# Depthwise convolution of two channel tiles by even and odd tokens, and adaLN sums in PSUM

## The chip, the cores and the metric

The kernel is written by hand for one core of a Trainium2 chip; the seven others are idle. The metric is the device time of one execution in microseconds (us). The core has a matrix engine (PE), a vector engine (DVE), an activation engine (ACT), a general engine (POOL) and a queue engine (SP), each with its own in-order instruction stream; they wait for each other by semaphores. SBUF is the on-chip memory of 128 partitions; PSUM is the smaller memory that PE writes, here eight banks of 128 x 512 fp32.

## The reference

One layer of a decoder trunk on 1024 tokens of width 1024, all in fp32:

```python
mod = silu(c) @ ada_w + ada_b                      # 1024 -> 6 x 1024
sh1, sc1, g1, sh2, sc2, g2 = split(mod, 6)
h = rms_norm(x, mix_pre_g) * (1 + sc1) + sh1
proj = h @ w_in          # q, k, v: 512 each; 8 gate logits; conv value, conv gate: 512 each
attn = fox_attention(q, k, v, log_sigmoid(f_logit + b_f))
u = conv_val * sigmoid(conv_gate)
u = causal_depthwise_conv(u, conv_w, conv_b)       # 31 taps, per channel, over tokens
u = silu(layer_norm(u, conv_ln_g, conv_ln_b))      # over the 512 channels
y = concat([attn, u]) @ w_o
x = x + g1 * rms_norm(y, mix_post_g)
h = rms_norm(x, ffn_pre_g) * (1 + sc2) + sh2
x = x + g2 * rms_norm(swiglu_ffn(h), ffn_post_g)   # 1024 -> 2 x 2816 -> 1024
```

The change touches the depthwise convolution and the first line, the product of one vector with the wide matrix `ada_w`.

## The kernel before

Channels lie on the partitions, tokens along the free axis. Every matrix product is three matmuls of two-part operands (`mm3`, L322 to L325): high times high, low times high, high times low. The parts are made by ACT (`whi`, L306) and DVE or POOL (`wlo`, `hTl`, L307).

The first 70 us follow a hand-written list of steps (`SEQ`, L37) that fixes the order on all five queues. In it the tokens are loaded, normalised and transposed (`xhat`, `ptx`), and the scale and shift of adaLN are made by column tiles of 128, for `j` from 0 to 7. `ada_load` brings a 128 x 8 x 2 x 128 piece of `ada_w` from DRAM through SP. `ada_sum` multiplies each of the 8 slices with a number per partition and adds them up on DVE into one or two running sums `adac` (L227, L229). `ada_turn` adds the partitions up by matmuls with a column of ones (`pada`, L239), and two small DVE operations make `acol` and `bcol`. With them ACT scales a tile of `h`, which is split and fed to the first projection matmuls (`pg`).

Then PE makes the projections: conv gate and value of channel tiles 1, 2, 3 (`conv_tile`, each gate and value tile two halves of 512 tokens), v, then k and q (`kq`), each into one of the five PSUM banks of `gbank`. Between conv tiles 1 and 2 stands `ada_row` (L283): the row form of the gate g1 in two halves of 512, each a sum of 8 slices on DVE (`adacr`, L196 and L198), one matmul with ones that sums the partitions (`padar`, L297) and two DVE operations into `g1b` (L299, L300).

The conv of a channel tile is 31 taps on two halves of 512 tokens (`conv_unit`): `csum += w[j] * u[j : j + 512]`. Of the eight units three are done by ACT (product `ctmp`, L413) and POOL (sum, L416) and five by DVE: a first product (L406) and 30 more operations (L409), whose running sum `csum` is one PSUM bank; the last tap writes the result `cacc` to SBUF. DVE's taps are given the lowest priority (`later`), so that the scheduler places them in gaps between other DVE work. POOL's and ACT's orders are by hand in this stage; those of DVE, PE and SP come from priorities.

From the projection of the last k and q tiles on, `conv_norm` transposes the four `cacc` of 128 tokens into a bank (`ptl`, L673), takes the statistics (`bs`, L676), aggregates them (`mv`, L678), makes the reciprocal deviation on POOL (L680) and normalises on DVE (`xn`, L682). `conv_silu` transposes back (`ptm`, L689). The banks of `ptl`, `ptm`, `ptx`, `padar` and `ptf` are the two of `tbank`. `ptf` (L563) transposes `lt`, the log of the forget gates, ahead of the second half of v, whose low parts DVE writes into `vv` (L593: per token and head 64 values, then 64 of the high part). The adaLN columns of the FFN (`ada_cols`, tiles `aacc`) are summed in the same stage in SBUF. Attention, `w_o` and the FFN follow and are not touched by the change, but that the FFN's `ada_row` uses the edited helper `ada_acc`.

## Time and profile before

| | us |
|---|---|
| runs | 1238.88, 1247.13, 1244.58 |
| median | 1244.58 |
| the profiled execution, its own time | 1241.7 |
| its span | 1239.8 |
| PE busy in the span | 1152.4 (93%) |
| DVE busy | 901.5 (73%) |
| POOL busy | 730.3 (59%) |
| ACT busy | 578.3 (47%) |

The span is the stretch of the profiled execution in which the engines worked; the execution's own time is 1.9 us longer, and the median of the runs is 2.9 us above it. The busy shares are means over stages of very different kinds: the first 70 us, the projections up to about 303 us, attention up to 445 us, then `w_o` and the FFN. The mean granted clock of PE is 0.973 of full speed.

### The profile page before, as it was taken

What the parts mean: (1) busy time and instruction counts of PE and PEld (TensorE: products, weight loads), DVE (VectorE), ACT (ScalarE), POOL (GpSimd) and SP (SyncE); (2) the same over time, 40 slices, a digit from 0 to 9 for tenths busy, and PEclk for the clock granted to TensorE, in tenths of its full rate; (3) what the DMA queues carried; (4) which work ended last, traced back from release to release, by engine and by line L of the source; (5) the groups of instructions that cost most, each with busy time, mean ns of one, the idle gap of its engine ahead of it and who ended that gap; (6) DMA issues with size and microseconds to landing.
All of it is one profiled execution on the core that took longest, in us unless ns stands there. A gap on an engine that the chain in (4) does not pass through costs nothing.

```text
span 1239.8 us, 16349 instructions
## 1 busy us (share of the span) xinstructions
PE 1152.4 (93%) x5517; PEld 949.1 (77%) x5517; DVE 901.5 (73%) x1395; ACT 578.3 (47%) x1084; POOL 730.3 (59%) x653
## 2 busy tenths in 40 slices
PE   4898989987799999898999999999999999999886
PEld 4676888876689977786788888888888877867565
DVE  4869899897598844548875656676665557597996
ACT  4654665363688845545433333333333244433451
POOL 3667878865667624565655545545455255456864
PEclk9999999988899999998899999999999999999999
DMA  9663102875966356412332332332313591444041
GB/s 300 178 221 86 35 18 70 233 236 173 287 176 168 100 167 196 136 51 89 119 119 69 98 103 81 124 98 81 102 56 107 191 358 46 157 148 144 31 149 68
DMA packets 177292, 166.41 MB, mean 134 GB/s; under 512 B 9789, under 2 KB 139153, under 8 KB 177208
## 3 DMA queue, kind: packets, MB, share of 16 engines
q1 hardware_dynamic: 158800, 151.62, 39.5%
q10 hardware_dynamic: 17096, 9.02, 2.6%
q0 software_dynamic: 1312, 4.72, 1.1%
q8 instruction: 44, 0.72, 0.2%
q14 instruction: 40, 0.33, 0.1%
HBM read 129.64 MB, written 33.06 MB: 131 GB/s over the span
## 4 chain that ended last, share of the span: by engine, by line
PE 61%; DVE 18%; POOL 7%; DMA 6%; issue 4%; ACT 3%; SPq 0%; POOLq 0%; ACTq 0%; DVEq 0%
PE mm L324 12%; PE mm L325 12%; PE mm L323 12%; PE m L324 4%; DVE wlo L307 4%; PE m L325 3%; PE m L323 3%; DVE csum L409 3%; PE pv L908 2%; PE pt L882 2%; DVE adac L229 2%; POOL cacc L416 2%; ACT whi L306 1%; PE sp L826 1%; PE sp L822 1%
## 5 line engine op out<-in xcount | busy, mean ns | idle before, releaser
L1116 POOL TENSOR_TENSOR sm<-raw 128x512 f32<-128x512 f32 x108 | 149.2, 1399 | 111.6 <-DVE fwl L307 93.8
L307 DVE TENSOR_TENSOR wlo<-raw,whi 128x512 fp32r<-128x512 f32 (+2 forms) x99 | 118.5, 1197 | 60.4 <-ACT whi L306 60.3
L416 POOL TENSOR_TENSOR cacc<-cacc,ctmp 128x512 f32<-128x512 f32 x90 | 128.4, 1427 | 28.3 <-ACT ctmp L413 21.8
L306 ACT CAST whi<-raw 128x512 fp32r<-128x512 f32 (+2 forms) x99 | 82.4, 834 | 125.2 <-PE m L325 50.6
L324 PE MATMUL m<-wlo,whi 128*128 128x512 f32 (+1 forms) x292 | 119.0, 407 | 17.8 <-DVE wlo L307 17.5
L306 ACT CAST fwh<-sm 128x512 fp32r<-128x512 f32 (+1 forms) x86 | 62.9, 731 | 132.3 <-PE mm L324 94.8
L325 PE MATMUL m<-whi,wlo 128*128 128x512 f32 (+1 forms) x292 | 114.7, 393 | 0.0
L323 PE MATMUL m<-whi 128*128 128x512 f32 (+1 forms) x292 | 114.0, 393 | 0.1
L409 DVE SCALAR_TENSOR_TENSOR csum<-u,cw,csum 128x512 f32<-128x512 f32 x145 | 108.9, 751 | 3.2
L1319 POOL TENSOR_TENSOR u<-u,g 128x512 f32<-128x512 f32 x42 | 61.7, 1469 | 79.9 <-ACT fwh L306 59.3
L323 PE MATMUL mm<-hTh,whi 128*128 128x512 f32 x224 | 90.9, 406 | 0.2 <-ACT whi L306 0.2
L324 PE MATMUL mm<-hTl,whi 128*128 128x512 f32 x224 | 90.7, 405 | 0.0
L325 PE MATMUL mm<-hTh,wlo 128*128 128x512 f32 x224 | 89.5, 402 | 0.0
L324 PEld LDWEIGHTS m<-wlo,whi 128*128 128x128 f32 x292 | 54.7, 187 | 43.5 <-DVE wlo L307 32.4
L413 ACT ACTIVATE ctmp<-u,cw 128x512 f32<-128x512 f32 x90 | 64.0, 723 | 43.9 <-POOL cacc L416 43.8
L307 DVE TENSOR_TENSOR fwl<-sm,fwh 128x512 fp32r<-128x512 f32 (+1 forms) x86 | 77.0, 896 | 10.0 <-ACT fwh L306 9.9
L1398 POOL TENSOR_TENSOR raw<-ablk,a 128x512 f32<-128x512 f32 x33 | 55.3, 1674 | 35.8 <-DVE wlo L307 34.3
L323 PEld LDWEIGHTS m<-whi 128*128 128x128 f32 x292 | 54.9, 188 | 13.5 <-DVE u L1316 0.5
L325 PEld LDWEIGHTS m<-whi,wlo 128*128 128x128 f32 x292 | 54.9, 188 | 11.1
L198 DVE SCALAR_TENSOR_TENSOR adacr<-adawr,cact,adacr 128x128 f32<-128x128 f32 (+1 forms) x70 | 60.6, 875 | 1.6
L842 POOL TENSOR_TENSOR nm<-nm,ones_n 128x1 f32<-128x1 f32 x64 | 39.2, 613 | 32.1 <-ACT pm L836 26.9
L1318 ACT ACTIVATE g<-g 128x512 f32<-128x512 f32 x44 | 27.7, 630 | 61.0 <-DVE g L1311 55.9
(349 smaller groups left out, 3495.6 us busy)
## 6 DMA issues: line engine op xcount, KB each, us to landing
raw<-in_w_ffn_in_dram SPq DMA_DIRECT2D x44, 512.0 KB, 3.6
bblk<-in_w_ffn_out_dram SPq DMA_DIRECT2D x55, 256.0 KB, 2.8
act_d<-u SPq DMA_DIRECT2D x42, 256.0 KB, 2.5
raw<-in_w_in_dram SPq DMA_DIRECT2D x18, 512.0 KB, 5.4
ablk<-act_d SPq DMA_DIRECT2D x33, 256.0 KB, 3.0
xt<-in_x_dram SPq DMA_DIRECT2D x16, 512.0 KB, 5.6
adaw<-in_ada_w_dram SPq DMA_DIRECT2D x16, 512.0 KB, 7.4
adaw<-in_ada_w_dram ACTq DMA_DIRECT2D x16, 512.0 KB, 3.9
```

Source lines behind the costliest of these rows:

```text
L198: nc.vector.scalar_tensor_tensor(acc, w[:, a], cact[:, a : a + 1], acc, ALU.mult, ALU.add)
L306: nc.scalar.copy(hi, raw)
L307: eng.tensor_tensor(lo, raw, hi.bitcast(F32), ALU.subtract)
L323: nc.tensor.matmul(ps, sh, mh, start=first, stop=False)
L324: nc.tensor.matmul(ps, sh, ml, start=False, stop=False)
L325: nc.tensor.matmul(ps, sl, mh, start=False, stop=last)
L409: eng.scalar_tensor_tensor(ps if j < CK - 1 else acc, us, w, ps, ALU.mult, ALU.add)
L413: nc.scalar.activation(tmp, us, AF.Copy, scale=w)
L416: eng.tensor_tensor(acc, acc, tmp, ALU.add)
L1116: nc.gpsimd.tensor_tensor(d, blk[o[0]], blk[o[2]], o[1])
L1319: (nc.vector if f == NF - 1 else nc.gpsimd).tensor_tensor(u, u, g, ALU.mult)
L1398: eng.tensor_tensor(sm[:, zs], blocks[c + o[0], k], blocks[c + o[2], k], o[1])
```

## The change

Two things change.

Conv tiles 2 and 3 are done by `conv_pair`. For even and odd tokens, with `a` the even taps' filter (16 taps) and `b` the odd taps' filter (15 taps), a 31-tap result of 1024 tokens is made of three filters: `a` on one half of the tokens (`pa`), `b` on the other (`pb`), and `a + b` on the sum of the two halves (`csm`). Each of the first two reads every second token of `u`. The even outputs are `pa + pb`; the odd outputs are the third filter less the two, built up in PSUM with the negated sums of taps, `cwn`. The last token is done alone by a small operation. `csum` gets two banks, so the projections' `gbank` gets four instead of five.

The running sums of adaLN go to PSUM: `ada_sum`'s into the same two banks as `csum` (`arun`), where `pada` now lives too, and `ada_row`'s into a bank of `tbank` (`adar`). Only the last operation of each sum writes SBUF. The mask of the first stage shares the space of `g1b`, and one scratch tile has a single buffer.

```diff
--- before.py
+++ after.py
@@ -94,6 +94,8 @@
     C_MP, C_AB, C_FP, C_CB, C_LG, C_LB = 0, 8, 56, 64, 68, 72
     bfb = cst.tile([P, NH], F32, name="bfb")
     cw = cst.tile([P, 4, CK], F32, name="cw")
+    cwn = cst.tile([P, 4, CK // 2], F32, name="cwn")
+    cbn = cst.tile([P, 4], F32, name="cbn")
     vT = cst.tile([P, NV], F32, name="vT")
     ab1 = cst.tile([P, 48], F32, name="ab1")
     cact = cst.tile([P, NK], F32, name="cact")
@@ -107,7 +109,7 @@
     stp, stp_es = pool("stp", 2)
 
     def gbank(name):
-        return psI.tile([P, 512], F32, tag="mm", name=name, bufs=5)
+        return psI.tile([P, 512], F32, tag="mm", name=name, bufs=4)
 
     def tbank(name):
         return psT.tile([P, 512], F32, tag="tr", name=name, bufs=2)
@@ -116,7 +118,7 @@
     crow = stp.tile([NK, P], F32, name="crow", bufs=1)
     vrows = stp.tile([C_FP, P], F32, name="vrows", bufs=1)
     vrows2 = stp.tile([NV - C_FP, P], F32, name="vrows2", bufs=1)
-    mask32 = stp.tile([P, P], F32, name="mask32", bufs=1)
+    mask32 = g1b[:, :P]
     nc.gpsimd.memset(mask32, 0.0)
     nc.gpsimd.affine_select(
         out=mask32, in_=mask32, pattern=[[-1, P]], compare_op=ALU.is_ge,
@@ -164,6 +166,9 @@
             pt = tbank("ptc")
             nc.tensor.transpose(pt[:, :CK], cwr[:, cb * P : (cb + 1) * P], ident[:CK, :CK])
             nc.vector.tensor_copy(cw[:, cb, :], pt[:, :CK])
+        nc.vector.scalar_tensor_tensor(
+            cwn, cw[:, :, 0 : CK - 1 : 2], -1.0, cw[:, :, 1::2], ALU.mult, ALU.subtract)
+        nc.vector.tensor_scalar(cbn, vT[:, C_CB : C_CB + 4], -2.0, 0.0, ALU.mult, ALU.add)
 
 
     xhat = stp.tile([P, NT, D], F32, name="xhat", bufs=1)
@@ -179,7 +184,7 @@
     def x_load(t):
         xt = xts[t] = stp.tile([P, D], F32, tag="xt", name="xt", bufs=3)
         nc.sync.dma_start(xt, xd[t * P : (t + 1) * P, :])
-        jk = stp.tile([P, D], BF16, tag="jk", name="jk")
+        jk = stp.tile([P, D], BF16, tag="jk", name="jk", bufs=1)
         nc.scalar.activation(jk, xt, AF.Square, accum_out=ss[:, t : t + 1])
         rstd_of(rstd[:, t : t + 1], ss[:, t : t + 1], D)
 
@@ -191,11 +196,13 @@
             nc.gpsimd.tensor_scalar(xhat[:, t, :], xt, rstd[:, t : t + 1], 0.0, ALU.mult, ALU.add)
 
 
-    def ada_acc(w, acc):
-
-        nc.vector.tensor_scalar_mul(acc, w[:, 0], cact[:, 0:1])
+    def ada_acc(w, acc, run=None):
+
+        run = acc if run is None else run
+        nc.vector.tensor_scalar_mul(run, w[:, 0], cact[:, 0:1])
         for a in range(1, NK):
-            nc.vector.scalar_tensor_tensor(acc, w[:, a], cact[:, a : a + 1], acc, ALU.mult, ALU.add)
+            nc.vector.scalar_tensor_tensor(
+                run if a < NK - 1 else acc, w[:, a], cact[:, a : a + 1], run, ALU.mult, ALU.add)
 
     acol = cst.tile([P, 2, NK], F32, name="acol")
     bcol = cst.tile([P, 2, NK], F32, name="bcol")
@@ -220,18 +227,21 @@
 
         w, npe, na = aw[j], int('40100000'[j]), int('22212111'[j])
         acc = stp.tile([P, 2, 2, P], F32, tag="adac", name="adac", bufs=2)
+        run = psI.tile([P, 512], F32, tag="cs", name="arun", bufs=2).rearrange("p (z m n) -> p z m n", z=2, m=2)
         aacc[j] = acc, na
         for a in range(npe, NK):
-            d = acc[:, (a - npe) % na]
+            z = (a - npe) % na
+            d = run[:, z]
             if a - npe < na:
                 nc.vector.tensor_scalar_mul(d, w[:, a], cact[:, a : a + 1])
             else:
-                nc.vector.scalar_tensor_tensor(d, w[:, a], cact[:, a : a + 1], d, ALU.mult, ALU.add)
+                nc.vector.scalar_tensor_tensor(
+                    d if a + na < NK else acc[:, z], w[:, a], cact[:, a : a + 1], d, ALU.mult, ALU.add)
 
     def ada_turn(j):
         acc, na = aacc.pop(j)
         w, npe = aw.pop(j), int('40100000'[j])
-        pt = gbank("pada")
+        pt = psI.tile([P, 512], F32, tag="cs", name="pada", bufs=2)
         for m in range(2):
             ops = [(w[:, a, m, :], cact[:, a : a + 1]) for a in range(npe)] + [
                 (acc[:, z, m], onesf[:, 0:1]) for z in range(na)]
@@ -291,7 +301,7 @@
             nc.sync.dma_start(br[:, 1], gvec[0:1, h * n : (h + 1) * n].broadcast_to([P, n]))
             yield
             acc = pl.tile([P, n], F32, tag="adac", name="adacr", bufs=2)
-            ada_acc(w, acc)
+            ada_acc(w, acc, bank("adar")[:, :n])
             yield
             pt = bank("padar")
             nc.tensor.matmul(pt[:, :n], onesf, acc, start=True, stop=True)
@@ -396,7 +406,7 @@
 
         acc = cvp.tile([P, 512], F32, tag=f"ca{cb}{h}", name="cacc", bufs=1)
         cacc[cb, h] = acc
-        ps = psI.tile([P, 512], F32, tag="cs", name="csum", bufs=1) if eng is nc.vector else None
+        ps = psI.tile([P, 512], F32, tag="cs", name="csum", bufs=2) if eng is nc.vector else None
 
         def tap(j):
             def f():
@@ -419,7 +429,41 @@
         for j in range(CK):
             put(tap(j))
 
+    def conv_pair(cb, u):
+
+
+
+        acc = cvp.tile([P, S], F32, tag=f"cq{cb}", name="cacc", bufs=1)
+        for h in range(2):
+            cacc[cb, h] = acc[:, HF[h]]
+        N, M = S // 2, CK // 2
+        pa, pb = [psI.tile([P, 512], F32, tag="cs", name="csum", bufs=2) for _ in range(2)]
+        sm = cvp.tile([P, N + M - 1], F32, tag="csm", name="csm", bufs=1)
+        bias = vT[:, C_CB + cb : C_CB + cb + 1]
+        w = lambda j: cw[:, cb, j : j + 1]
+        at = lambda j, n=N: u[:, j : j + 2 * n - 1 : 2]
+        v = nc.vector
+        later(v.tensor_scalar, pa, at(0), w(0), bias, ALU.mult, ALU.add)
+        for j in range(2, CK, 2):
+            later(v.scalar_tensor_tensor, pa, at(j), w(j), pa, ALU.mult, ALU.add)
+        later(v.tensor_scalar, pb, at(1), w(1), 0.0, ALU.mult, ALU.add)
+        for j in range(3, CK, 2):
+            later(v.scalar_tensor_tensor, pb if j < CK - 2 else acc[:, 0::2], at(j), w(j), pb, ALU.mult, ALU.add)
+        later(v.tensor_tensor, sm, at(1, N + M - 1), at(2, N + M - 1), ALU.add)
+        pb = pb[:, : N - 1]
+        later(v.scalar_tensor_tensor, pb, pa[:, 1:], cbn[:, cb : cb + 1], acc[:, 0 : S - 2 : 2], ALU.add, ALU.add)
+        later(v.tensor_tensor, acc[:, 0::2], pa, acc[:, 0::2], ALU.add)
+        for i in range(M):
+            later(v.scalar_tensor_tensor, pb, sm[:, i : i + N - 1], cwn[:, cb, i : i + 1], pb, ALU.mult, ALU.add)
+        later(v.scalar_tensor_tensor, acc[:, 1 : S - 1 : 2], sm[:, M : M + N - 1], w(CK - 1), pb, ALU.mult, ALU.subtract)
+        jk = cvp.tile([P, CK], F32, tag="cjk", name="cjk", bufs=1)
+        later(lambda: v.tensor_tensor_reduce(
+            out=jk, in0=u[:, S - 1 : S - 1 + CK], in1=cw[:, cb, :], scale=1.0, scalar=bias,
+            op0=ALU.mult, op1=ALU.add, accum_out=acc[:, S - 1 : S]))
+
     def conv_taps(cb, u):
+        if cb >= 2:
+            return conv_pair(cb, u)
         for h in range(2):
             if (cb, h) in POOL_UNITS:
                 conv_unit(cb, h, u, nc.gpsimd, pool_work.append)
```

Three places in the order of the instructions follow. In the rows `mm` is a projection bank and `padar` the matmul that sums the partitions of an `adacr`; numbers behind names are tiles' numbers.

On PE, around the second `padar`; before, it stands in the second half of the gate projection of conv tile 2 (`mm_916`), 34 matmuls behind the first `padar`:

```order
L324 MATMUL mm_916<-hTl_100,whi_748 128x512
L325 MATMUL mm_916<-hTh_99,wlo_749 128x512
L323 MATMUL mm_916<-hTh_99,whi_748 128x512
L297 MATMUL padar_870<-adacr_861,onesf_77 128x512
L324 MATMUL mm_916<-hTl_100,whi_748 128x512
L325 MATMUL mm_916<-hTh_99,wlo_749 128x512
L323 MATMUL mm_916<-hTh_99,whi_748 128x512
```

With the change, in the first half of the value projection of conv tile 2 (`mm_970`), 55 matmuls behind the first:

```order
L334 MATMUL mm_970<-hTl_102,whi_913 128x512
L335 MATMUL mm_970<-hTh_101,wlo_914 128x512
L333 MATMUL mm_970<-hTh_101,whi_913 128x512
L307 MATMUL padar_883<-adacr_873,onesf_77 128x512
L334 MATMUL mm_970<-hTl_102,whi_913 128x512
L335 MATMUL mm_970<-hTh_101,wlo_914 128x512
L333 MATMUL mm_970<-hTh_101,whi_913 128x512
```

The second `padar` has moved 21 matmuls back; the first stands where it stood.

On DVE, from the second half of conv tile 1's `u` on, before: the second sum of `adacr` had begun ahead of it, with three of its eight operations done:

```order
L198 SCALAR_TENSOR_TENSOR adacr<-adawr,cact,adacr 128x512
L409 SCALAR_TENSOR_TENSOR csum<-u,cw,csum 128x512
L383 TENSOR_TENSOR u<-mm,sg 128x512
L299 TENSOR_TENSOR g1b<-padar,adab 128x512
L198 SCALAR_TENSOR_TENSOR adacr<-adawr,cact,adacr 128x512
L300 TENSOR_TENSOR g1b<-g1b,adab 128x512
L198 SCALAR_TENSOR_TENSOR adacr<-adawr,cact,adacr 128x512
L307 TENSOR_TENSOR wlo<-raw,whi 128x1024
L198 SCALAR_TENSOR_TENSOR adacr<-adawr,cact,adacr 128x512
L409 SCALAR_TENSOR_TENSOR csum<-u,cw,csum 128x512
L198 SCALAR_TENSOR_TENSOR adacr<-adawr,cact,adacr 128x512
L409 SCALAR_TENSOR_TENSOR csum<-u,cw,csum 128x512
```

With the change:

```order
L416 TENSOR_SCALAR csum<-u,cw,vT 128x512
L419 SCALAR_TENSOR_TENSOR csum<-u,cw,csum 128x512 x5
L393 TENSOR_TENSOR u<-mm,sg 128x512
L309 TENSOR_TENSOR g1b<-padar,adab 128x512
L202 TENSOR_SCALAR adar<-adawr,cact 128x512
L310 TENSOR_TENSOR g1b<-g1b,adab 128x512
L204 SCALAR_TENSOR_TENSOR adar<-adawr,cact,adar 128x512
L317 TENSOR_TENSOR wlo<-raw,whi 128x1024
L204 SCALAR_TENSOR_TENSOR adar<-adawr,cact,adar 128x512
L419 SCALAR_TENSOR_TENSOR csum<-u,cw,csum 128x512
L204 SCALAR_TENSOR_TENSOR adar<-adawr,cact,adar 128x512
L419 SCALAR_TENSOR_TENSOR csum<-u,cw,csum 128x512
```

The second sum (now `adar`) begins with its first product (L202) behind `u` and the first `g1b`; its remaining operations alternate with taps as before.

On DVE, at the end of the conv, before: the transposes' first statistics (`BN_STATS`) and what follows, with taps of the last tile behind them:

```order
L307 TENSOR_TENSOR wlo<-raw,whi 128x1024
L645 SCALAR_TENSOR_TENSOR tql<-mm,tq 128x512
L409 SCALAR_TENSOR_TENSOR csum<-u,cw,csum 128x512 x9
L632 TENSOR_TENSOR tl<-mm,th 128x512
L409 SCALAR_TENSOR_TENSOR csum<-u,cw,csum 128x512
L676 BN_STATS bs<-ptl 128x6 x2
L196 TENSOR_SCALAR aacc<-adaw_2385,cact 128x128
L678 BN_AGGR mv<-bs 128x2 x2
L198 SCALAR_TENSOR_TENSOR aacc<-adaw_2385,cact,aacc 128x128
L409 SCALAR_TENSOR_TENSOR csum<-u,cw,csum 128x512
```

With the change:

```order
L475 SCALAR_TENSOR_TENSOR csum<-csm,cwn,csum 128x511 x6
L676 TENSOR_TENSOR tl<-mm,th 128x512
L475 SCALAR_TENSOR_TENSOR csum<-csm,cwn,csum 128x511 x2
L317 TENSOR_TENSOR wlo<-raw,whi 128x1024
L475 SCALAR_TENSOR_TENSOR csum<-csm,cwn,csum 128x511 x3
L689 SCALAR_TENSOR_TENSOR tql<-mm,tq 128x512
L475 SCALAR_TENSOR_TENSOR csum<-csm,cwn,csum 128x511
L475 SCALAR_TENSOR_TENSOR cacc<-csm,cw,csum 128x511
L317 TENSOR_TENSOR wlo<-raw,whi 128x1024
L689 SCALAR_TENSOR_TENSOR tql<-mm,tq 128x512
L676 TENSOR_TENSOR tl<-mm,th 128x512
```

Before, 16 taps of the last unit stand behind the first `BN_STATS`, alternating with the sums `aacc`; now the last tap (`cacc`) stands ahead of it.

## Rows read from the trace of the kernel before

**Rows 1.** Windows: length; busy of PE, PEld, DVE, ACT, POOL; clock; DMA share, GB/s.
```profile
0.00:46.00 46.00, 28.10 (x114) 23.59 (x115) 28.66 (x66) 23.20 (x36) 20.96 (x36) 0.96 1.09 305
46.00:70.00 24.00, 22.10 (x119) 17.50 (x117) 15.03 (x23) 16.07 (x25) 14.68 (x11) 1.00 0.31 99
70.00:102.00 32.00, 31.65 (x135) 24.87 (x135) 27.98 (x31) 16.72 (x24) 25.32 (x17) 1.00 0.57 173
102.00:113.00 11.00, 5.23 (x15) 3.24 (x14) 10.26 (x12) 2.89 (x4) 8.36 (x6) 0.84 0.58 166
113.00:260.00 147.00, 143.66 (x807) 125.05 (x807) 132.42 (x189) 80.75 (x137) 121.15 (x93) 0.99 0.35 98
260.00:303.00 43.00, 32.49 (x143) 25.92 (x143) 39.13 (x79) 22.14 (x56) 21.56 (x31) 0.80 0.60 184
445.00:1240.00 795.00, 755.88 (x3268) 606.34 (x3266) 537.04 (x700) 306.39 (x546) 423.42 (x318) 0.98 0.36 119
```

**Rows 2.** Waits of PE, 70 to 310 us: total, times, longest.
```profile
PE padar L297 <- DVE adacr L198: 5.8, 1, 5.8
PE ptl L673 <- DVE cacc L409: 3.9, 1, 3.9
PE ptl L673 <- DVE xn L682: 3.5, 1, 3.5
PE ptf L563 <- DVE lt L558: 3.3, 1, 3.3
PE ptm L689 <- DVE xn L682: 3.0, 2, 2.7
```

**Rows 3.** Waits of PE, 10 to 70 us, the column matmuls.
```profile
PE pada L239 <- DVE adac L229: 7.3, 5, 3.5
```

**Rows 4.** Timeline of DVE: start, length, operation, two chains of column sums.
```profile
16.71 2.45 DVE L229 SCALAR_TENSOR_TENSOR adac<-adaw,cact,adac 128x256 f32<-128x256 f32 x6
...
45.84 8.46 DVE L229 SCALAR_TENSOR_TENSOR adac<-adaw,cact,adac 128x256 f32<-128x256 f32 x7
```

**Rows 5.** Lines of DVE by form, 70 to 112 us: busy, mean ns.
```profile
L198 DVE SCALAR_TENSOR_TENSOR adacr<-adawr,cact,adacr 128x512 f32<-128x512 f32 x14 | 17.6, 1255 | 0.2
L307 DVE TENSOR_TENSOR wlo<-raw,whi 128x1024 fp32r<-128x1024 f32 x4 | 6.3, 1575 | 3.4 <-ACT whi L306 3.4
L409 DVE SCALAR_TENSOR_TENSOR csum<-u,cw,csum 128x512 f32<-128x512 f32 x8 | 6.0, 745 | 0.0
...
L300 DVE TENSOR_TENSOR g1b<-g1b,adab 128x512 f32<-128x512 f32 x2 | 2.5, 1234 | 0.0
L383 DVE TENSOR_TENSOR u<-mm,sg 128x512 f32<-128x512 f32 x2 | 1.4, 684 | 0.3 <-PE mm L325 0.3
L299 DVE TENSOR_TENSOR g1b<-padar,adab 128x512 f32<-128x512 f32 x2 | 1.4, 682 | 0.7 <-PE padar L297 0.7
```

**Rows 6.** Tile `cacc` on POOL: min/median/max ns, first and last start.
```profile
L416 POOL TENSOR_TENSOR cacc<-cacc,ctmp x90: 1266/1299/2800, 72.4 to 228.1; 128x512 f32<-128x512 f32 x90
```

**Rows 7.** Tile `adac` on DVE, the column sums of the first stretch.
```profile
L229 DVE SCALAR_TENSOR_TENSOR adac<-adaw,cact,adac x47: 472/484/1582, 11.3 to 60.7; 128x256 f32<-128x256 f32 x47
L227 DVE TENSOR_SCALAR adac<-adaw,cact x12: 332/351/1379, 10.8 to 55.4; 128x256 f32<-128x256 f32 x12
```

**Rows 8.** Tile `adaw`: issues of the column loads on SP, first and last start.
```profile
L215 SPq DMA_DIRECT2D adaw<-in_ada_w_dram x16: 368/1296/3642, 1.6 to 39.1; - x16
```

**Rows 9.** DMA issues, 0 to 60 us: KB each, median us to landing.
```profile
adaw<-in_ada_w_dram SPq DMA_DIRECT2D x16, 512.0 KB, 7.4
```

**Rows 10.** Tile `csum`: the first taps, which write PSUM.
```profile
L406 DVE TENSOR_SCALAR csum<-u,cw,vT x5: 812/814/815, 89.4 to 244.8; 128x512 f32<-128x512 f32 x5
```

**Rows 11.** Lines of DVE by form, 112 to 290 us: taps, an eviction of v.
```profile
L409 DVE SCALAR_TENSOR_TENSOR csum<-u,cw,csum 128x512 f32<-128x512 f32 x137 | 102.9, 751 | 3.1
...
L593 DVE TENSOR_TENSOR vv<-mmv,vv 128x256 fp32r<-128x256 f32 x16 | 6.7, 416 | 2.3 <-ACT vv L592 2.3
```

**Rows 12.** Timeline of DVE: one operation of 1024 elements.
```profile
272.09 1.21 DVE L307 TENSOR_TENSOR wlo<-raw,whi 128x1024 fp32r<-128x1024 f32 x1
```

## The prediction

> **What bounds the kernel now.** I read the windows first [rows 1]. From 445 us to the end PE is busy 755.88 of 795 us, and from 113 to 260 us 143.66 of 147. Vector work that this change saves inside those stretches gives nothing back there: PE is the bound, at a granted clock of 0.98 and 0.99. The stretches in which PE is short of work are four: 0 to 46 us (28.10 busy), 46 to 70 (22.10 of 24), 102 to 113 (5.23 of 11, clock 0.84) and 260 to 303 (32.49 of 43, clock 0.80). DVE is busy 28.66, 15.03, 10.26 and 39.13 us in them.
>
> The list of what PE waited for says who ends these gaps [rows 2]. At 102 to 113 it is one wait of 5.8 us: the row matmul `padar` on the sum `adacr` that DVE had not finished. At 260 to 303 there are waits of 3.9 (the last conv tap, `cacc`), 3.5 and 3.0 us (`xn`), 10.4 together, all DVE, and 43 − 32.49 = 10.5 us are idle. Between them stands one of 3.3 us (`ptf` on `lt`). In the first 70 us PE waits 7.3 us in five pieces for the column sums `adac` [rows 3]. So nearly all PE idle time that the change can touch is ended by DVE, and by the operations that it edits.
>
> Last I looked at prices. DVE has two for the same work. Six sums of 128x256 beginning at 16.71 us took 2.45 us, 0.41 each; seven at 45.84 took 8.46, 1.21 each [rows 4]. The row sums `adacr`, 128x512, mean 1255 ns, while conv taps of the same size which accumulate in PSUM mean 745 ns in the same stretch [rows 5]. Both kinds read one SBUF tensor and one running sum; the slow kind has its sum in SBUF, and POOL works then: its adds run from 72.4 us on, about 1.3 us each [rows 6].
>
> **The change, part by part.**
>
> *Column sums in PSUM (first 70 us).* 47 sums of 128x256 (median 484 ns, up to 1582) and 12 first products (median 351) [rows 7] write a PSUM bank instead; only the last of each chain writes SBUF. Their price I bound by the half of a conv tap, 0.745/2 = 0.37, and by today's isolated 0.48; I take 0.42. The seven at 45.84 would then take 2.9 us, 5.6 less. But most of that meets another limit: the 16 loads are issued until 39.1 us and land 7.4 us later [rows 8, 9], so the last sum can't begin before about 46.5 us, and from 46 to 70 PE is idle only 1.9 us. What can be got is this 1.9, and of the 7.3 us of waits those that a load does not set. The first bank is shared by the sums and by the matmuls that total them, so PE's second `pada` now waits for DVE's first chain; its reader stands behind that chain on DVE anyway, and I cost it at nothing (cover gone: one chain of 8 × 0.42 = 3.4 us). I take −3.5 us; ends 0 and −6.
>
> The row for a first product shows 351 ns for 256 elements, less than the 472 that the fastest sum takes. The Trainium skill, "VectorE: DVE Perf Modes", section "Why PSUM operands drop a tier", says that an operand in PSUM excludes the doubled fp32 mode, which speaks against this edit. By it the 12 products would lose the doubling, 4.2 us, and the sum below would be −12 at worst, were all of it on the path. The nearest row that writes PSUM, a `tensor_scalar` of 128x512 in 814 ns [rows 10], makes 0.41 of 256 elements, 0.06 more than now, 0.7 us for the 12; I take the row, and it lies behind the loads.
>
> *Row sums in PSUM (85 to 113 us).* 16 operations of 128x512 (14 sums of 1255 ns and two first products, taken alike) go to about 0.75 and 0.81 us [rows 5, 10]: 8 us less DVE work. The order moves too: the second `padar` stands 55 matmuls behind the first instead of 34. PE does a matmul in 31.65/135 = 0.234 us [rows 1], so it arrives 21 × 0.234 = 4.9 us later in its own order, with useful work done before. DVE's chain now begins behind the second `u`: 0.68 (`u`) + 0.68 (`g1b`) + 0.81 (first product) + 1.23 (`g1b` again) + 1.58 (`wlo`) + 7 sums and 5 taps between them × 0.75 = 14.0 us [rows 5, 10]. PE needs 55 × 0.234 = 12.9 us from the first `padar`, whose end nearly coincides with the release of `u`. So about 1 us of wait is left of 5.8. The half clock behind the wait costs today 11 × 0.16 = 1.8 us (0.84 granted) and mostly goes. −4.9 −0.6 = −5.5 us; ends 0 (the sums stay at 1.25: 7 × 0.5 = 3.5 longer, with half clock after it) and −6.5.
>
> *Two conv tiles by pairs.* Per tile 62 taps of 128x512 become 31 with a step of two, one sum, two joins, 15 taps on that sum, a last one with a stepped write and one tiny sum: 51. At 0.751 [rows 11] 22 fewer are −16.5 us of DVE work. In 113 to 260 it hides: PE is at 143.66 of 147. What counts is the order: before, 16 taps, 12 us, stand behind the first BN_STATS, and four transposes `ptl` wait for the last; now all taps stand ahead of it. Ahead of it there are still 22 − 16 = 6 fewer than before, 4.5 us, plus the 8 us of row sums. So `cacc` no longer ends a wait (3.9), and `xn` is queued behind 12 us fewer taps (6.5 us of waits). Not all goes: between `bs` and `xn` lies a step on POOL, the normalisation has only two banks, and one projection bank of five is given up. The clock of 0.80 comes from these gaps. I take −7 us (two thirds of 10.4); ends −3 and −9.5 (all of the waits less 1 us for the lost bank).
>
> *`ptf`.* The same DVE operations stand ahead of `lt`: 0, ends −1 and +4 (a whole stall more).
>
> *Queues.* On SP the loads of the v and k weights change places, on POOL and ACT a few steps of attention. PE's list of waits up to 310 us [rows 2] names no load, POOL or ACT that comes so late: 0; without that cover it is case A.
>
> *The rest*, attention and FFN: same sums of 128x128, PE-bound: 0, −1 to +1. The two tiny sums of filters: under 0.4 us on DVE at 70 us, where `wlo` follows; 0.
>
> The sum is −3.5 −5.5 −7 = −16 us, on a profiled execution of 1241.7 us: 1225.7. The median of the runs, 1244.58, is 2.9 us above that one, so 1228.6 on its footing; I say **1227**. Its own range is 1219 to 1233.
>
> **The rivals.**
>
> *A. The stall comes back elsewhere.* PE, released earlier, meets the next late thing: the loads in the first 46 us (DMA at 1.09 of a full share [rows 1]), four projection banks, ACT's casts, or POOL's taps, 90 adds ending after 228.1 us [rows 6], which the change does not shorten. For it: the loads run without a pause. Against: every long wait listed names DVE. Half of the gain: −1, −3.5, −3.5: −8, **1236** (1232 to 1241). Chance 0.20.
>
> *B. A step of two costs time (the other side).* No row of before reads or writes every second element. If the engine passes 1024 elements to take 512, an operation costs what the 128x1024 `wlo` at 272.09 us costs, 1.21 [rows 12], 0.46 more than a tap. 34 stepped operations per tile are then 31 us against 16.5 saved: 14.8 us more DVE work, in a stretch where DVE has 147 − 132.42 = 14.6 us free, most of it while it waits. The conv would end up to 15 us later than today, and with it the transposes: instead of −7 there stands +8 to +15. With the −9 of the other parts 1244 to 1251 on the median; **1248**. It decides from about 0.4 us per operation (68 × 0.4 − 16.5 = 10.7, more than the other parts give). Against it speaks the nearest row that leaves elements out: the eviction into `vv` writes blocks of 64 and skips 64 after each, and its 256 elements took 416 ns [rows 11], where the same operation takes 684 for 512 without gaps (`u` [rows 5]), so the skipped ones cost little or nothing. It is no step of two, and so B keeps a chance: 0.08.
>
> The Trainium skill, "Advanced Engine Details and Errata", section "SBUF Cachelines", gives lines of 16 bytes and asks for two hits on a line for full speed; every second fp32 value makes two hits, so by it B does not happen, and no row here shows it.
>
> *C. The vector work was hidden anyway*, and only the row matmul moves: −5.5 and nothing else, with a wait of 3.5 us more at `ptf`: 1241 to 1245. Against: 10.4 us of waits. Chance 0.06.
>
> **How the numbers follow.** The forecast has 0.64; A 0.20, B 0.08, C 0.06; 0.02 are for luck beyond. The range 1219 to 1241 holds the forecast but for its tail, and A: about 0.82. One per cent, 12.4 us, is about what can be told from no change here, so faster means under 1232.1 and slower over 1257.0. The forecast lies under 1232.1 in nearly all of its range (0.62), A in a little of its own (0.03): faster 0.65. B goes beyond 1257 only with ends added (0.03), and 0.01 for luck: slower 0.04. The rest, 0.31, is same.
>
> **What would show it.** Right: stepped taps at 0.75 us; `padar` with a wait near 1 us; no wait of `ptl` on `cacc`; the stretch of the last kq tiles up to attention shorter by about 7 us, at a clock above 0.85; sums of 128x256 near 0.42 with POOL at work; PE's span from 113 to 260 as dense as before. Wrong: taps above 1.1 us (B); the waits renamed to a DMA, ACT or POOL (A); `ptf` above 6 us (C). A wait on the shared bank that outlives DVE's chain, or attention starting no earlier although the waits are gone, would make the prediction wrong in a way that none of the cases has.

## The result, and the profile after

The changed kernel takes 1229.19 us (median of 4 runs, 1222.98 to 1231.55) where the kernel before takes 1242.49 (1238.88 to 1247.13): a ratio of 0.987, with a 95% interval of 0.9831 to 0.9909. On another chip it was timed once more: 0.9855 (0.9832 to 0.9879). The forecast was 1227 us, from a sum of −16; measured are −13 to −18. The total was right, but by luck, since its parts were not: the adaLN sums in PSUM earned more than I gave them, the change of banks some, and the conv pairs, for which I had written down 7 us, nothing that can be measured.

Beside the times one yardstick serves throughout: when PE starts certain matmuls in the profiled execution (us; a step is the time from the column ahead). `ptc` transposes the conv's taps at the end of the first stage, `mmv` is the bank of v, `py` that of the output projection.

| kernel | `ptc`, end of first stage | first `padar` | first `mmv` (v) | `ptf` | first `ptl` | first `py` (`w_o`) | span |
|---|---|---|---|---|---|---|---|
| before | 69.8 | 93.6 | 147.6 | 182.0 | 255.0 | 449.1 | 1239.8 |
| changed | 62.9 | 86.4 | 132.3 | 169.0 | 242.5 | 432.0 | 1227.2 |
| each step, changed less before | −6.9 | −0.3 | −8.1 | +2.3 | +0.5 | −4.6 | +4.5 |

The same windows of the changed kernel (columns as in [rows 1]):

```profile
0.00:46.00 46.00, 30.80 (x139) 25.90 (x140) 27.18 (x68) 27.58 (x43) 23.14 (x39) 1.00 1.10 301
46.00:70.00 24.00, 23.65 (x123) 19.24 (x122) 14.06 (x32) 14.63 (x22) 15.07 (x12) 1.00 0.53 162
70.00:102.00 32.00, 32.00 (x137) 25.42 (x136) 24.27 (x33) 19.53 (x28) 27.00 (x20) 1.00 0.45 139
102.00:113.00 11.00, 11.00 (x49) 9.02 (x49) 9.39 (x15) 5.86 (x8) 10.45 (x8) 1.00 0.69 194
```

PE does 139 instead of 114 matmuls in the first 46 us, at a clock of 1.00 instead of 0.96, and the hole at 102 to 113 us is gone. What PE still waits for, from 70 to 310 us and, below, from 10 to 70 us (there without a wait of `pv` for a load, 7.2 us, before 6.4; `bcol` took 1.3 before). `tl` is the low part of a half of k, `tq` and `tql` are the high and low part of a half of q; they are stored to DRAM in `qk_d`:

```profile
PE ptf L607 <- DVE lt L602: 5.2, 1, 5.2
PE pada L287 <- DMA qk_d<-tql: 5.2, 1, 5.2
PE mm L333 <- DVE tl L676: 2.6, 1, 2.6
...
PE ptl L717 <- DVE tql L689: 0.9, 1, 0.9
PE mm L333 <- DVE tql L689: 0.5, 1, 0.5
```

```profile
PE pada L249 <- DVE adac L238: 2.6, 2, 2.4
PE pada L249 <- DVE bcol L215: 2.2, 2, 1.4
```

Against [rows 2, 3], `padar` has left the list, and so has the wait of `ptl` on `cacc`; but `ptf` waits 5.2 us instead of 3.3, and the late stage has new names: `tl`, `tql` and a store, 9.2 us where 10.4 stood. In the second trace of the changed kernel the store is not among them: `tl` 3.5, `aacc` 2.4, a load of `ncum` 1.8, `tql` 1.6.

The operations themselves, by form on DVE, first the adaLN row sums from 70 to 112 us, then the conv from 112 to 240 us:

```profile
L204 DVE SCALAR_TENSOR_TENSOR adar<-adawr,cact,adar 128x512 f32<-128x512 f32 x11 | 8.2, 748 | 0.1
...
L204 DVE SCALAR_TENSOR_TENSOR adacr<-adawr,cact,adar 128x512 f32<-128x512 f32 x2 | 1.5, 742 | 0.0
```

```profile
L475 DVE SCALAR_TENSOR_TENSOR csum<-u,cw,csum 128x512 f32<-128x512 f32 x56 | 40.1, 746 | 0.3
L475 DVE SCALAR_TENSOR_TENSOR csum<-csm,cwn,csum 128x511 f32<-128x511 f32 x30 | 22.4, 747 | 0.4
...
L475 DVE TENSOR_TENSOR csm<-u 128x526 f32<-128x526 f32 x2 | 2.9, 1471 | 0.0
```

A row sum fell from 1255 to 748 ns, the same whether its last operation writes PSUM or SBUF. A tap with a step of two takes 746 ns, as one without (751 [rows 11]). Both prices of the forecast hold, and rival B is out. The one sum that reads two SBUF tensors, `csm`, takes 1471 in the mean (1.14 and 1.81 us). In the first stage six column sums beginning at 44.45 us, where before seven took 8.46 us [rows 4]:

```profile
44.45 3.12 DVE L238 SCALAR_TENSOR_TENSOR arun<-adaw,cact,arun 128x256 f32<-128x256 f32 x6
```

They are 0.52 us each, not the 0.42 I took. The row nearest to that, six in 2.45 us [rows 4], is two sums in SBUF that take turns; two that take turns in one PSUM bank also follow each other every 0.52 us (four in 2.06 us from 16.85).

### The profile page after: what moved, and what is told of

It reads as the page before. It is cut to its first block, busy times and chain, and to the rows that moved or that the text cites. A ratio compares the mean times of both kernels' runs of the same rounds, so it can differ in the third digit from the quotient of the medians.

```text
span 1227.2 us, 16335 instructions
## 1 busy us (share of the span) xinstructions
PE 1145.2 (93%) x5517; PEld 947.3 (77%) x5517; DVE 852.1 (69%) x1377; ACT 577.7 (47%) x1084; POOL 726.9 (59%) x653
## 4 chain that ended last, share of the span: by engine, by line
PE 58%; DVE 14%; POOL 12%; DMA 6%; issue 5%; ACT 4%; SPq 0%; POOLq 0%; ACTq 0%; DVEq 0%
PE mm L333 11%; PE mm L334 11%; PE mm L335 11%; POOL cacc L426 5%; PE m L334 4%; PE m L335 3%; PE m L333 3%; DVE wlo L317 3%; PE pt L926 2%; PE pv L952 2%; DMA adaw<-in_ada_w_dram 2%; DMA raw<-mixA 2%; DVE csum L475 1%; ACT whi L316 1%; PE sp L870 1%
## 5 line engine op out<-in xcount | busy, mean ns | idle before, releaser
L317 DVE TENSOR_TENSOR fwl<-sm,fwh 128x512 fp32r<-128x512 f32 (+1 forms) x86 | 83.2, 969 | 14.6 <-ACT fwh L316 14.4
L926 PE MATMUL pt<-ident,pm 128*128 128x128 f32 x288 | 46.4, 279 | 8.9 <-DVE pl L941 6.5
L333 PEld LDWEIGHTS mm<-hTh,whi 128*128 128x128 f32 x224 | 42.5, 190 | 13.8 <-DVE tl L676 2.8
```

The costliest lines, as they stand in the source:

```text
L317: eng.tensor_tensor(lo, raw, hi.bitcast(F32), ALU.subtract)
L333: nc.tensor.matmul(ps, sh, mh, start=first, stop=False)
L926: nc.tensor.transpose(pt[:, c * P : (c + 1) * P], self.u.pms[q][:, (self.b0 + bb) * P : (self.b0 + bb + 1) * P], ident)
```

## The experiments

The theory after the result: each part of the change pays in its own stage, and only where PE stood waiting for DVE. The rival: the relief of DVE as a whole, above all by the pairs, made the gain. The first four kernels take the change apart; they were timed together, in 3 rounds against the kernel before (1246.17 us there).

**Pairs only.** Changed kernel, with the sums back in SBUF:

```diff
-        run = psI.tile([P, 512], F32, tag="cs", name="arun", bufs=2)...
...
-            d = run[:, z]
+            d = acc[:, z]
...
-            ada_acc(w, acc, bank("adar")[:, :n])
+            ada_acc(w, acc)
```

> The changed kernel with the adaLN sums back in SBUF (arun and adar gone, pada in the two banks of csum, four projection banks): only the conv pairs are left. Theory, that each part pays in its own stage: the first stage ends where it ended before (PE's turn of the second rows at 69 to 70 us, not 62.9), PE waits 5 to 6 us for the second padar again, the sums adacr mean about 1.25 us, ptl waits on no tap; of the 13 us about 4 to 5 remain, so 1237 to 1239. Rival, that the relief of DVE by the pairs made the whole gain: 1229 to 1231 and a first stage as short as in the changed kernel.

Measured: 1242.13 us, ratio 0.9975 (0.9956 to 0.9994). First stage to 70.0 us. Its waits:

```profile
PE pada L248 <- DVE adac L237: 8.6, 5, 3.6
...
PE padar L306 <- DVE adacr L204: 6.3, 1, 6.3
...
PE ptf L606 <- DVE lt L601: 5.1, 1, 5.1
PE sp L865 <- DVE tql L688: 2.5, 1, 2.5
PE pada L286 <- DVE aacc L204: 2.4, 1, 2.4
PE mm L332 <- DVE tl L675: 1.7, 1, 1.7
PE ptl L716 <- DVE xn L725: 1.5, 1, 1.5
```

The early waits are all back: the pairs do nothing for them. The rival is out; but the time also missed the 1237 to 1239 of the theory, and even the 3 us left turn out not to be the pairs' (four banks, below).

**Sums only.** Changed kernel, all conv tiles by 31 taps:

```diff
     def conv_taps(cb, u):
-        if cb >= 2:
-            return conv_pair(cb, u)
```

> The changed kernel with all four conv tiles by 31 taps: the sums in PSUM and the four banks stay. Theory: first stage ends near 62.9 us, second padar without a wait, v's first matmul 15 us earlier than before (about 132 us); the waits of ptl on the last tap and on xn (10 us before) stay or grow, since 22 taps more lie on DVE: 1232 to 1236. Rival, that the pairs are worth nothing because DVE's work in 113 to 260 us is hidden: 1228 to 1230.

Measured: 1227.42 us, ratio 0.9854 (0.9814 to 0.9893), the same as the changed kernel with its pairs (0.9855, timed with the later kernels). My own theory expected 1232 to 1236 and missed; what its "rival" said of the pairs came true. First stage 63.3, `mmv` 133.4, `py` 432.1: PE begins the output projection at the same place, to 0.1 us, with and without the pairs. The pairs do relieve DVE: with them its last tap ends at 233.6 us, 9 us ahead of the first `ptl`, without them at 263.3. It gains nothing. The late waits:

```profile
PE sp L864 <- DVE tql L687: 2.9, 1, 2.9
...
PE ptl L715 <- DVE tql L687: 2.6, 2, 1.4
PE mm L333 <- DVE tl L674: 2.2, 1, 2.2
...
PE ptl L715 <- DVE xn L724: 1.4, 2, 0.9
```

No wait on `cacc`, although taps stand behind the first `BN_STATS` again: five, where the kernel before has 16 (four banks, below).

**Column sums only.** As the last, with the row sums in SBUF:

```diff
-            ada_acc(w, acc, bank("adar")[:, :n])
+            ada_acc(w, acc)
```

> As the last, and the row sums in SBUF again: only the column sums of the first stage are in PSUM. Theory: the first stage ends at 63 us (7 us earlier than before) and nothing else is earlier; the second padar has its wait of about 6 us back, and v's first matmul stands at about 140 us: 1235 to 1239. Rival, that the first stage is bound by its loads and the gain there is that of the later stage seen early: 69 us and 1241 to 1243.

Measured: 1238.36 us, ratio 0.993 (0.9909 to 0.9951). First stage 65.3 us, `padar` waits 6.4 us again, `mmv` at 144.1. Time and wait are as the theory had it; the first stage ends 2.3 us and `mmv` stands 4 us later than it said. The quotient to the kernel with both sums, 0.9854/0.993 = 0.9923, puts the row sums at 9.5 us, by the two intervals some 4 to 15; in the traces the step from the first `padar` to `mmv` is 55.2 us here and 46.3 with both sums.

**Four banks only.** Kernel before, with the changed kernel's banks:

```diff
-        return psI.tile([P, 512], F32, tag="mm", name=name, bufs=5)
+        return psI.tile([P, 512], F32, tag="mm", name=name, bufs=4)
...
-        pt = gbank("pada")
+        pt = psI.tile([P, 512], F32, tag="cs", name="pada", bufs=2)
...
-... name="csum", bufs=1)
+... name="csum", bufs=2)
```

> The kernel before with the banks of the changed one: four for the projections, two for csum and pada; nothing else. Theory: the fifth bank costs at most 1 us, so 1241 to 1244, the first stage ends at 69 to 70 us. Rival, that pada's separate bank is what sped up the first stage: it ends under 67 us. Rival, that the lost bank costs some of the gain: 1245 to 1249, with new waits of PE on the operations that empty the banks.

Measured: 1242.28 us, ratio 0.9976 (0.9958 to 0.9995): no cost, rather 3 us of gain, and the same as the pairs with these banks (0.9975). First stage 69.9 us, so the separate bank did not speed it up. Its late waits:

```profile
PE mm L323 <- DVE tl L632: 3.4, 1, 3.4
...
PE sp L822 <- DVE tql L645: 2.9, 1, 2.9
PE ptl L673 <- DVE tql L645: 2.8, 2, 1.6
PE pada L277 <- DVE aacc L198: 1.7, 1, 1.7
```

This kernel has none of the sums and none of the pairs, and yet the waits on `cacc` are gone. The scheduler places the late work otherwise, and the waits take other names; they make 10.8 us. Two things of the edit meet here. `ptl` takes its bank from `gbank`, as `mm` does, and not from `tbank`, as is said ahead of the prediction; so it stands in line with q's projections for one bank less, and waits 2.8 us on `tql`. And `csum` has a second bank, so that taps of two units can take turns. Six taps of the kernel before, in one bank, and 15 of this kernel:

```profile
142.78 4.71 DVE L409 SCALAR_TENSOR_TENSOR csum<-u,cw,csum 128x512 f32<-128x512 f32 x6
```

```profile
129.39 9.96 DVE L409 SCALAR_TENSOR_TENSOR csum<-u,cw,csum 128x512 f32<-128x512 f32 x15
```

They follow each other every 0.66 us instead of 0.79. From start to start the conv's taps hold DVE for 106 us instead of 118, and four of them stand behind the first `BN_STATS` instead of 16. So it is most likely this second bank that does what the pairs were to do for the wait on `cacc`; no run has it alone. From first `ptl` to first `py` it needs 194.1 us, as the kernel before. Where its 3 us (by the interval 0.6 to 5.2) come from is open: up to `py` its trace is 1.1 us ahead, and behind it 5.7 us longer than the trace of before.

From these four and the changed kernel, each against the one with a part less: banks 0.9976 (−3.0 us); columns 0.993/0.9976 (−5.7); rows 0.9923 (−9.5); pairs 0.9855/0.9854 (0). Reckoned so, one from the other, they make the −18 of 0.9855 whatever the parts are; that they add up confirms nothing. The intervals leave about 2.3 us either way on the banks, 3.5 on the columns, 5.6 on rows and on pairs. For the pairs there is a second value that does not depend on it: pairs only against banks only, 0.9975 and 0.9976.

**What the wait at `ptf` costs.** The next kernels were timed together in 5 rounds (before: 1247.07 us), the changed kernel among them:

> The changed kernel once more, on the same chip as the next ones. Theory, that the pairs add nothing to the sums in PSUM: 1228 to 1232, its ratio to before within 0.003 of the kernel without pairs (0.9854). Rival, that they add the 7 us of the forecast: ratio below 0.981. In its trace the stretch of the output projection is 106 to 109 us long, as in the other runs with four banks, and the 103.4 us of before's profile were a short one.

Measured: 1229.27 us, 0.9855 (0.9832 to 0.9879): the theory.

`fturn` holds the transposes, the scan and the store:

```diff
+        return lt
+
+    def fturn(lt):
...
-            fgate()
+            lt = fgate()
...
+            if g == 1 and t == 6:
+                fturn(lt)
```

> The changed kernel with the two groups of transposes ptf of the forget gates called before the seventh token tile of v's second half instead of ahead of the first: 77 matmuls of 0.12 us, 9 us, later on PE. Theory: the wait of 5.2 us and the half clock behind it (0.83 of 17 us, 2.9 us) go, so first ptl comes 7 to 8 us earlier; after it part is lost to the transfers of the last k and q tiles: 3 to 8 us faster than the changed kernel. Rival, that the stall moves to those transfers whole: no faster than the changed kernel by more than 1 us.

Measured: 1224.59 us, ratio 0.9822 (0.9803 to 0.9841), 4.7 us less than the changed kernel. From 132 to 186 us (windows) PE has no hole, and the clock is whole:

```profile
132.00:169.00 37.00, 37.00 (x304) 36.84 (x303) 32.94 (x63) 23.60 (x41) 29.64 (x24) 1.00 0.06 15
169.00:186.00 17.00, 17.00 (x121) 15.82 (x120) 16.75 (x28) 11.09 (x19) 16.14 (x12) 1.00 0.02 4
```

The changed kernel stood for more than half of the 9 us ahead of `ptf`, and had 0.83 of the clock behind it:

```profile
160.00:169.00 9.00, 3.80 (x32) 3.60 (x30) 8.07 (x20) 6.80 (x12) 3.98 (x5) 0.94 0.00 0
169.00:186.00 17.00, 16.98 (x121) 16.39 (x122) 15.24 (x23) 8.37 (x16) 13.64 (x11) 0.83 0.02 4
```

First `ptl` is at 236.7 us, 4.4 to 5.8 ahead of the changed kernel's two traces, less than the 7 to 8 expected; `py` is 3.2 ahead. Behind `ptl` the wait on `tl` grew to 5.7 us (2.6 and 3.5 in the two traces), and `pada` waits 4.4 for the store of `tql` (5.2 in the one, none in the other): part of the gain was handed on.

**The same without pairs.** This was to show whether the pairs pay once PE comes earlier.

> The last kernel with all four conv tiles by 31 taps: sums in PSUM, four banks, late ptf. Theory, that the pairs add nothing as long as PE has no wait that they end: within 2 us of the last kernel. Rival: with PE's order 8 us tighter ahead of the transposes, DVE's 22 more taps are late for them, and it is 4 to 8 us slower than the last kernel, with waits of ptl on cacc.

Measured: 1225.75 us, 0.9835 (0.9816 to 0.9855): 1.2 us from the last, the intervals overlap. The third comparison with and without pairs, and the third without a difference.

**Fewer loads.** Changed kernel, 13 of the 16 loads for `ada_cols` left out:

```diff
+                if i >= 3:
+                    w[i] = keep[i % 3]
+                    return
...
```

> The changed kernel, but of the 16 loads of 512 KB for the FFN's adaLN columns (227 to 302 us) only the first three are made, and their tiles are used again, so that the column values are not those of the reference; the work of the engines on them stays. Theory, that the waits of the last k and q tiles are set by the DMA queues (share 0.77 and 0.93 from 242 to 300 us): from first ptl to the first matmul of the output projection 4 us or more less than 189.5, and the wait of pada on the store of tql goes. Rival, that DVE's and ACT's order sets them: less than 2 us.

Measured: 1229.53 us, 0.9874 (0.9846 to 0.9902). From `ptl` to `py` 194.8 us, longer, not shorter. The theory gets no support, but the run does not refute it either. ACT's wait for the store of `tq` fell, from 15.3 us in the changed kernel (10.9 in its second trace):

```profile
ACT tq L687 <- DMA qk_d<-tq: 15.3, 2, 14.1
```

to 6.0, while DVE now waits 10.6 us for POOL's products, which are made in the few tiles again and again:

```profile
DVE aacc L202 <- POOL adaw L283: 10.6, 2, 8.6
```

The edit set up a new wait of its own. The next one tests the same idea without that.

**Two buffers for what is stored.** Kernel with late `ptf` and without pairs (SBUF has room there), in 5 rounds (before: 1245.67 us):

```diff
-            tq = qkt.tile([P, 512], F32R, tag="tq", name="tq", bufs=1)
+            tq = qkt.tile([P, 512], F32R, tag="tq", name="tq", bufs=2)
...
-            ql = qkt.tile([P, 512], F32R, tag="tql", name="tql", bufs=1)
+            ql = qkt.tile([P, 512], F32R, tag="tql", name="tql", bufs=2)
...
-        xn = lnp.tile([P, 512], F32, tag="xn", name="xn", bufs=3)
+        xn = lnp.tile([P, 512], F32, tag="xn", name="xn", bufs=2)
```

> The kernel with late ptf and no pairs, with two buffers for tq and tql, which wait for their own stores, and two instead of three for xn (SBUF has no room for more): Theory, that the stores of the last q tiles set the start of attention: from first ptl to the first matmul of the output projection 4 us or more less than 193.9, total 1218 to 1223. Rival, that the stores only stand in line on the DMA queues whichever buffer they come from: within 2 us of the kernel with late ptf and no pairs.

Measured: 1220.43 us, ratio 0.980 (0.9771 to 0.983), the lowest of all; by the ratios that is 4.4 us less than without the second buffers, though the two were timed on different chips and their intervals just overlap. `ptl` to `py` took 185.5 us instead of 193.9, less than in any other trace (188.8 to 194.8). The gain lies in attention (windows from its first matmul to `py`, without and with the second buffers):

```profile
295.80:431.30 135.50, 122.96 (x865) 113.48 (x865) 110.41 (x294) 110.30 (x260) 87.56 (x131) 0.94 0.61 158
```

```profile
297.20:424.30 127.10, 119.58 (x865) 111.03 (x865) 109.51 (x291) 106.37 (x253) 87.78 (x131) 0.97 0.64 169
```

ACT's wait for the store of `tq` (9.4 us) and DVE's for that of `tql` (2.9) are gone, the last store is issued 57.4 us behind the first `ptl` instead of 62.5, and in its first 30 us attention does 168 matmuls instead of 113. So in the stage where I had put the pairs' 7 us, single buffers held by stores were one bound; DVE's taps were not. Whether the pairs would pay beside second buffers no run shows.

**What makes a sum slow.** Kernel before, with POOL's three units cut to their first tap (timed once, as the two that follow):

```diff
-        for j in range(CK):
+        for j in range(CK if ps is not None else 1):
             put(tap(j))
```

> The kernel before, with POOL's three conv units cut to their first tap (90 products of ACT and 90 adds of POOL left out; the conv's values are not the reference's). Theory, that a sum with both inputs in SBUF is lengthened by POOL's work: the row sums adacr take 0.75 us instead of 1.25, and PE's wait for the second padar falls from 5.8 to under 2 us. Rival, that a running sum in SBUF is slow of itself: 1.25 us and 5 to 6 us as before.

Measured: 1231.25 us, and no wait at `padar`; `mmv` at 139.8 us.

```profile
L198 DVE SCALAR_TENSOR_TENSOR adacr<-adawr,cact,adacr 128x512 f32<-128x512 f32 x14 | 10.5, 747 | 0.2
```

The same instruction, both inputs in SBUF, takes 747 ns without POOL's taps and 1255 beside them [rows 5]. This run leaves out ACT's products too, so ACT could be the cause as well; the trace of before tells the two apart. Four of its sums stand ahead of an add for which POOL had idled 3.76 us:

```profile
76.63 3.11 DVE L198 SCALAR_TENSOR_TENSOR adacr<-adawr,cact,adacr 128x512 f32<-128x512 f32 x4
```

```profile
79.81 1.30 POOL L416 TENSOR_TENSOR cacc<-cacc,ctmp 128x512 f32<-128x512 f32 x1 [3.76 <-ACT ctmp L413]
```

They took 0.75 us each, the last of them wholly beside ACT's work. The nine sums that began while an add was running ended 0.55 us after that add's end, each of them, so they took 1.09 to 1.78 us. The slow price is a wait for POOL, and PSUM is a way out of it. POOL gains as well, though rival A said of its adds that the change does not shorten them: from 70 to 112 us they took 1568 ns in the mean before and 1409 with the change.

**Is the first stage still DVE's?** Changed kernel, four of the eight slices left out in six of the eight column tiles:

```diff
-        for a in range(npe, NK):
+        NE = NK if npe else NK // 2
+        for a in range(npe, NE):
...
```

> The changed kernel, with only four of the eight slices of each column tile from the second on summed in the first stage (the other four are loaded and left out, so that scale and shift are not the reference's): some 2 us less on DVE for each of seven tiles. Theory, that the first stage is now bound by PE and the loads: PE's turn of the second rows at 61.5 to 63 us (62.9 in the changed kernel). Rival, that DVE's sums still set it: 57 to 60 us.

Measured: first stage to 64.6 us, no shorter. From 40 to 63 us PE has no hole, and DVE now waits for PE:

```profile
40.00:63.00 23.00, 23.00 (x130) 19.32 (x129) 5.78 (x17) 16.41 (x25) 15.40 (x12) 1.00 0.59 150
```

```profile
56.79 0.22 DVE L211 SCALAR_TENSOR_TENSOR acol<-pada,ab,vT 128x1 f32<-128x1 f32 x1 [3.63 <-PE pada L250]
```

So shorter column sums give nothing more. The end of the first stage lies between 62.9 and 65.5 us in the traces of all kernels with these sums in PSUM, so its gain is 4 to 7 us; single traces do not tell it closer.

**A step of four.** Changed kernel, the first filter's taps on 256 elements with a step of four, the second's on 260 with a step of two:

```diff
-            later(v.scalar_tensor_tensor, pa, at(j), w(j), pa, ALU.mult, ALU.add)
+            later(v.scalar_tensor_tensor, pa[:, :256], u[:, j : j + 1021 : 4], w(j), pa[:, :256], ALU.mult, ALU.add)
...
+                later(v.scalar_tensor_tensor, pb[:, :260], at(j, 260), w(j), pb[:, :260], ALU.mult, ALU.add)
...
```

> The changed kernel, with the taps of the first filter cut to 256 elements read with a step of four (each on a 16-byte line of its own) and those of the second filter to 260 elements read with a step of two; the conv's values are not the reference's. Theory, cost by elements taken: both forms the same, 0.42 to 0.50 us. Rival, that a line touched only once costs more: the 256 elements with a step of four take 0.6 us or more, the 260 with a step of two 0.42 to 0.50.

Measured, by form from 112 to 240 us:

```profile
L478 DVE SCALAR_TENSOR_TENSOR csum<-u,cw,csum 128x256 f32<-128x256 f32 x30 | 20.6, 685 | 0.0
L478 DVE SCALAR_TENSOR_TENSOR csum<-u,cw,csum 128x260 f32<-128x260 f32 x26 | 12.8, 492 | 0.3
```

The rival was right: 256 elements with a step of four take 685 ns, 260 with a step of two 492. So a step can cost, one further on than here; but not as rival B had it: the 1024 elements that the 256 are taken from would then be passed in 1.21 us. The 685 against 492 ns is as the Trainium skill has it in "Advanced Engine Details and Errata", section "SBUF Cachelines": a line of 16 bytes that is hit only once costs, two hits are enough.

## Why the prediction was right in sum and wrong in its parts

*Column sums, −3.5 forecast.* Measured −6.9 in the first trace, −5.7 by the times. The step that failed is "What can be got is this 1.9, and of the 7.3 us of waits those that a load does not set". I counted PE's idle time behind 46 us and set too little for what lies ahead of it. Of the waits on `adac` 2.6 us are left, so 4.7 went (`bcol` took back 0.9); and I did not count the clock at all, though the row of 0 to 46 us showed 0.96 and now shows 1.00. The loads set less than I thought: PE did 25 more matmuls in the same 46 us. From 40 to 63 us PE is dense (23.00 us busy, before 21.10). The first products, for which I took 0.41 us from a row against 0.70 by the doubled mode that falls away, took 0.49 where they had taken 0.35 [rows 7]:

```profile
39.40 0.49 DVE L236 TENSOR_SCALAR arun<-adaw,cact 128x256 f32<-128x256 f32 x1 [2.35 <-DMA adaw<-in_ada_w_dram]
```

The Trainium skill, "VectorE: DVE Perf Modes", section "Why PSUM operands drop a tier", names such a loss. The trace agrees in the direction, but 0.49 to 0.35 is 1.4 times and not 2, some 0.14 us for each of the 12.

*Row sums, −5.5 forecast.* Measured −8.1 from the first `padar` to `mmv` in the trace, −9.5 by the times. The mechanism was right, and with it the second `padar`'s new place; the chain was sized at 14.0 us and took 12.0 (from `u` at 86.98 to the end of the last sum at 98.99). `g1b` takes 0.68 in it instead of 1.23, since this time POOL's add beside it is the one that was lengthened (1.85 us instead of 1.30), and sums and taps in turn follow each other every 0.66 us, not 0.75. So no wait of 1 us is left, the clock is 1.00 in the stretch, and 5.8 + 1.8 us came back whole; of the 1.8 the sum had taken 0.6, though it said that they "mostly" go.

*Pairs, −7 forecast.* Wrong: no difference in three comparisons. What failed is the way from "What counts is the order: before, 16 taps, 12 us, stand behind the first BN_STATS, and four transposes `ptl` wait for the last" to "I take −7 us (two thirds of 10.4)". The order was read rightly, and the wait on `cacc` did go, but it goes without the pairs too, with the banks alone, and the time stays: in that kernel 10.8 us of waits on `tl`, `tql` and `aacc` stand where 10.4 stood. That "the normalisation has only two banks" was misread in part: `ptl` shares the projections' banks. A list of waits names what came last; I took the sum of one engine's waits for a gain that follows when that engine is relieved. From `ptl` to `py` the changed kernel is 4.6 us faster than before in its first trace and 3.1 in the second, the one without pairs 2.9; what may be left for the pairs, 0.2 to 1.7 us, is lost at `ptf`, which is 1.8 us later with them (36.7 and 36.8 against 34.9 us from `mmv` on). The sign named for them, a shorter stretch up to attention, is there without them too: from first `ptl` to the first `sp` 56.9 and 55.1 us with pairs, 55.0 without, 61.4 before. That was rival C, for the pairs alone, and rival A in its stage: the transfers, as the second buffers bear out.

*`ptf`, 0 forecast (−1 to +4).* +1.9 by the wait. The DVE operations ahead of `lt` are not quite the same: the wait is 5.1 to 5.3 us in the traces with the pairs and 3.1 to 3.8 without them. *One bank less, up to 1 us of loss.* No loss, 3 us of gain by the times, unexplained.

*The rest, 0 (−1 to +1).* In the first traces the changed kernel loses 4.5 us behind `py`, 4.9 of it in `w_o`: 108.3 us from its first to its last matmul instead of 103.4. That stretch took between 102.6 and 109.2 us in the traces of the eleven experiments that don't edit it, and 108.4 in the second trace of the changed kernel; the only trace of before is a short one. So I put it to the run, not to the change; that before is long too in most runs was not seen, since there is one trace of it.

The errors were +2.2 and +4.0 us too little for the sums, 3 for the banks, and 7 too much for the pairs: they nearly cancel, and that the forecast met the time is luck. The rivals: B is excluded by the 746 ns, A holds in the last stage, C for the pairs.

## What to carry to other kernels

Before crediting a cheaper algorithm with an engine's waits, take it alone: here 22 operations fewer on two tiles, at the right price and in the right place, were worth nothing that could be measured; behind them stood single buffers that waited for their stores. A second accumulator bank, so that two sums take turns, took nearly as much time from DVE (12 us, 118 to 106) as the cheaper algorithm on top of it (14, 106 to 92). A sum that reads two SBUF tensors beside a busy POOL can be had at 0.6 of its price by keeping the running sum in PSUM, and that is worth most where PE waits for its last operation. Where a wait only changes its name when you remove it, look for the buffer that is held by a store.

## What the runs showed of the hardware

A sum of DVE with two SBUF inputs waits for a POOL add that is running: 128x512 takes 747 ns with POOL idle, 1255 in the mean beside POOL's adds, and one that begins inside an add ends 0.55 us after it. With the running sum in PSUM it does not wait (748 beside the same adds). Reading every second fp32 value is free (746 ns for 512), every fourth costs 1.4 times as much for about the same number of elements (685 ns for 256 against 492 for 260). Taps of 128x512 that add to one PSUM bank follow each other every 0.79 us; with two banks in turn it is 0.66. Sums of 128x256 in one bank follow each other every 0.52 us.
